# Attention queries and norm scales: which engine writes them

## The chip, the cores and the metric

The kernel runs on one core of a Trainium2 chip. A core has TensorE (PE, matrix products into PSUM), VectorE (DVE), ScalarE (ACT), GpSimd (POOL) and the queue engine SyncE (SP), each with an instruction queue of its own that it works off in order, with semaphores between them. The metric is the device time of one execution in microseconds (us). Lower is better.

## The reference

The reference is a two-layer transformer block for diffusion: 256 tokens of `x` and 256 tokens of context, model width 1024, all in float32.

- In each layer the tokens are normalized, modulated (AdaLN), and projected by one wide matrix `w_in` into four attention branches and their gates: windowed attention (8 heads of 64, 2 key heads), differential attention (4 heads of two 64-wide halves), neighbourhood attention (8 heads of 64, with a bias), and a low-rank attention (MLA, 8 heads of 64+32).
- Queries and keys of the heads are RMS-normalized per head: `y = x * rsqrt(mean(x*x) + 1e-6) * g`. The same formula normalizes the low-rank latents, the outputs of the differential branch and the tokens before each half of a layer.
- Each branch computes `softmax(q k^T * scale) v`; the four results are multiplied by `w_branch`, gated, summed and multiplied by `w_out`, and added to the tokens.
- A mixture of 16 experts follows (2 experts a token, chosen inside one of 4 groups): `(silu(x w1) * (x w3)) w2`, weighted and added.
- The last layer computes queries for the 256 tokens of `x` alone.

## The kernel before

**Numbers in two parts.** Projections keep float32 accuracy by splitting both operands into a high part (rounded to the fast float32 format, F32R) and a low part (what the rounding left), and adding three products (`mm3`, lines 284 to 288). ACT writes the high part (`whi`, line 274 or 308) and DVE, in the experts sometimes POOL, the low part by a subtraction (`wlo`, lines 275, 310, 312). There are 4 such pairs for the weights.

**Attention scores in two products.** For the windowed, differential and neighbourhood branches two heads of 64 share the 128 rows of a tile. The keys are prepared per head: 64 rows hold the high part of the head's keys and the other 64 rows hold their low part (`qk_post`, lines 761 and 762). The queries are prepared per unit (a pair of heads and 128 queries) by `heads` (lines 919 to 930). For each of the two heads, ACT writes the high part of the head's queries into the head's own 64 rows (line 927), POOL copies these 64 rows to the other 64 (line 928, through `QX` and `pmul` of line 261), and POOL writes the low part (line 929). One product of 128 rows then gives high times high plus high times low, and a second one adds low queries times high keys. The tiles rotate through 3 buffers (`qp`). There are 72 such units (16 a branch in layer 0, 8 in layer 1), hence 144 of each of the three instructions. MLA has its own form (lines 1114 and 1115), without the copy.

**One unit of attention.** PE computes the scores into two PSUM banks (line 773); DVE adds masks and finds the negated maximum (lines 778 to 785); ACT computes exp with its sum (line 787); DVE takes the reciprocal (line 792); POOL multiplies the probabilities by it (lines 810 and 856, shown as line 261 with tile `pp`); PE transposes (line 281), ACT and DVE by turns copy the result out of PSUM (lines 269 and 271), and PE multiplies by the values (lines 827 and 870).

**The norms.** `norm_heads` squares on ACT (line 711), sums on DVE (line 713), and calls `rstd_of` (lines 616 to 620): POOL computes sum times scale plus epsilon (line 618), then raises it to the power -0.5 (line 619). DVE multiplies (line 715). Where the square is summed by ACT's accumulator (lines 875, 1045, 1046, 1184, 2111), `rstd_of` stands behind ACT directly. In the output projection, `finish` does the same in two halves (lines 1381, 1382 and 1393). `rstd_of` is called 110 times, and line 1382 runs 12 times.

**Order of the work.** SP's queue, which starts the weight loads, keeps the written order. The instructions of the other engines are put in order at build time by a scheduler that goes by priority in written order and by its own estimate of each instruction's time; each engine then works off a fixed list. `run_main` (line 470) writes one branch's projection steps interleaved with the attention units of the branch before (`side`) and the norms of the heads (`posts`), so that PE has projections to do while a unit waits. Tiles of 128x512 that hold projected heads, squares and probabilities share 12 buffers (`t2`).

Of the kernel before, what the change touches and what calls it, by code (L numbers as in the profile page):

```python
# [13 lines left out]
AF = mybir.ActivationFunctionType  # L14
OP = mybir.AluOpType
# [5 lines left out]
D = 1024  # L21
# [4 lines left out]
EPS = 1e-6  # L26
# [184 lines left out]
def kernel(ctx: ExitStack, tc: tile.TileContext, a, out, dbg=None, depth=L):  # L211
# [9 lines left out]
    act = nc.scalar.activation  # L221
    V = nc.vector
    G = nc.gpsimd
# [8 lines left out]
    def psS(i):  # L232
        return psp.tile([P, 512], F32, name=f"S{i}", tag=f"S{i}", bufs=1)
# [13 lines left out]
    def t2(name="t2"):  # L247
        return gp.tile([P, 512], F32, name=name, tag="t2", bufs=BUFS["t2"])
# [4 lines left out]
    def small(n=8):  # L253
        return gp.tile([P, n], F32, name="sml", tag=f"sml{n}", bufs=16)
# [5 lines left out]
    def pmul(o, i, s, s2=1.0):  # L260
        G.tensor_scalar(o, i, s, s2, op0=OP.mult, op1=OP.mult)  # L261

    QX = lambda o, i: pmul(o, i, 1.0)
    ev = [0]

    def evac(o, i):
        ev[0] += 1
        if ev[0] % 2:
            act(o, i, AF.Copy)
        else:  # L270
            V.tensor_copy(o, i)
# [5 lines left out]
    def transposes(src, kts):  # L277

        pt = psT()
        for k, kt in enumerate(kts):  # L280
            tp(pt[:, k * P:(k + 1) * P], src[:, kt * P:(kt + 1) * P], ident)  # L281
        return pt
# [11 lines left out]
    def C(name):  # L294
        o, w = CSO[name]
        return cst[:, o:o + w]
# [318 lines left out]

    def rstd_of(ss, n, scale):
        r = small()[:, :n]
        G.tensor_scalar(r, ss, scale, EPS, op0=OP.mult, op1=OP.add)  # L618
        G.tensor_tensor(r, r, nhalf[:, :n], op=OP.pow)  # L619
        return r  # L620

# [60 lines left out]
    def attention_layer(l, T, hT):  # L682
# [24 lines left out]
        def norm_heads(x, H, hd, ct, stt, rot0):  # L707

            sq = t2("sq")
            sqv = sq[:, :H * hd].rearrange("p (h d) -> p h d", h=H)  # L710
            act(sqv, x, AF.Square)
            ss = small()
            V.tensor_reduce(ss[:, :H], sqv, axis=AX.X, op=OP.add)  # L713
            r = rstd_of(ss[:, :H], H, 1.0 / hd)
            V.tensor_tensor(x, x, r[:, :, None].to_broadcast([P, H, hd]), op=OP.mult)
            if stt is not None:
                rd = hd - rot0
                swv = sq[:, :H * rd].rearrange("p (h s d) -> p h s d", h=H, s=2)
                xr = x[:, :, rot0:].rearrange("p h (s d) -> p h s d", s=2)
                G.tensor_tensor(swv, xr[:, :, ::-1, :],  # L720
                                stt.rearrange("p (s d) -> p s d", s=2)[:, None].to_broadcast([P, H, 2, rd // 2]), op=OP.mult)
                G.tensor_tensor(x, x, ct[:, None, :].to_broadcast([P, H, hd]), op=OP.mult)
                V.tensor_tensor(x[:, :, rot0:], x[:, :, rot0:], sq[:, :H * rd].rearrange("p (h d) -> p h d", h=H), op=OP.add)
            else:
                V.tensor_tensor(x, x, ct[:, None, :].to_broadcast([P, H, hd]), op=OP.mult)
# [119 lines left out]
        def dif_slots(operands, Vt, yT):  # L845
# [20 lines left out]
            def pv(h, t):  # L866
                nb, kt0 = (4, 0) if t < 2 else (2, 2)
                po = psT()
                for b in range(nb):
                    mm(po[:, :P], PT[h, t][:, b * P:(b + 1) * P], Vt[:, kt0 + b, h * P:(h + 1) * P], start=b == 0, stop=b == nb - 1)  # L870
                o = do[:, t % 2]
                sq = t2("sq")[:, 0:P]
                ss = small()
                V.tensor_copy(o, po[:, :P])
                act(sq, o, AF.Square, accum_out=ss[:, 0:1])
                r = rstd_of(ss[:, 0:1], 1, 1.0 / P)
                V.scalar_tensor_tensor(o, o, r, S("sub"), op0=OP.mult, op1=OP.mult)
                O[h, t] = o
# [40 lines left out]
        def heads(q, k, ring):  # L919


            *qs, l0, l1 = ring[0]
            ring.append(ring.pop(0))
            ql = (l0, l1)
            for i in range(2):
                r, x = slice(i * 64, i * 64 + 64), slice(64 - i * 64, 128 - i * 64)
                act(qs[i][r], q[r], AF.Copy)
                QX(qs[i][x], qs[i][r])
                G.tensor_tensor(ql[i][r], q[r], qs[i][r], op=OP.subtract)
            return [[(i, v[i], k[i], g == 0, g == 1) for i in range(2)] for g, v in enumerate((qs, ql))]  # L930

        def stage_win():
# [31 lines left out]
            def slots():  # L964
                ring = padded()

                def ops(pi, tok, ks):
                    return heads(w["qT"].rearrange("p (b n) -> p b n", b=4)[:, pi, tok], [v[:, ks] for v in w["kT"]], ring)
                return std_slots(ops, lambda b, pi, i: w["V"][:, b, i * 64:(i + 1) * 64], y_of(0), range(4), sink=True, mask=True)
            return steps, slots  # L970

        def stage_qkv(pre, gq, gk, br):
# [20 lines left out]
            def ops(pi, tok, ks):  # L993
                return heads(w["qT"].rearrange("p (b n) -> p b n", b=4)[:, pi, tok],
                             [v.rearrange("p (b n) -> p b n", b=4)[:, pi, ks] for v in w["kT"]], w["ring"])
# [30 lines left out]
        def stage_mla():  # L1026
# [14 lines left out]
            def p1(t):  # L1041
                n = nats["ma", t]
                sq = t2("sq")
                ss = small()
                act(sq[:, :256], n[:, :256], AF.Square, accum_out=ss[:, 0:1])
                act(sq[:, 256:384], n[:, 256:384], AF.Square, accum_out=ss[:, 1:2])
                V.tensor_scalar(ss[:, 0:1], ss[:, 0:1], 0.5, None, op0=OP.mult)
                r = rstd_of(ss[:, 0:2], 2, 1.0 / P)
                V.scalar_tensor_tensor(n[:, 0:256], n[:, 0:256], r[:, 0:1], S("mqa"), op0=OP.mult, op1=OP.mult)
                V.scalar_tensor_tensor(n[:, 256:384], n[:, 256:384], r[:, 1:2], S("mkva"), op0=OP.mult, op1=OP.mult)  # L1050
                V.tensor_copy(w["kr"][:, t, :], n[:, 384:416])
# [129 lines left out]
    for t in range(4):  # L1181
        xn = t4("xn")
        ss = small()
        act(xn, xts[t], AF.Square, accum_out=ss[:, 0:1])
        r = rstd_of(ss[:, 0:1], 1, 1.0 / D)
# [56 lines left out]
    for l in range(depth):  # L1242
# [87 lines left out]
        for half in range(2):  # L1330
            for t in QT:
                pt = transposes(mt[t], range(half * 4, half * 4 + 4))
                o = [hT[i][:, half * 4:half * 4 + 4, t * P:(t + 1) * P] for i in range(2)]
# [37 lines left out]
        def finish(t, j, ps):  # L1371

            s = t // 2
            if j == 0:
                sss[t] = small()
            ss = sss[t]
            tmp, sq = t2("tmp"), t2("sq")
            cs = slice(j * 512, (j + 1) * 512)
            V.scalar_tensor_tensor(tmp, ps, 0.5, g1[s][:, cs], op0=OP.mult, op1=OP.mult)
            V.tensor_tensor(xt[t][:, cs], xt[t][:, cs], tmp, op=OP.add)  # L1380
            act(sq, xt[t][:, cs], AF.Square, accum_out=ss[:, j:j + 1])
            G.tensor_scalar(ss[:, 2 + j:3 + j], ss[:, j:j + 1], 1.0 / D, ss[:, 2:3] if j else EPS, op0=OP.mult, op1=OP.add)
            if t not in lgp:
                lgp[t] = psS(t % 2)
            pt = transposes(xt[t], range(j * 4, j * 4 + 4))
            xT = t2("xT")
            act(xT, pt, AF.Copy)
            for g in range(4):
                mm(lgp[t][32 * g:32 * g + 32, 0:P], rwA[:, j * 4 + g].rearrange("p s e -> p (s e)"), xT[:, g * P:(g + 1) * P],
                   start=j == 0, stop=j == 1, tile_position=(0, 32 * g))  # L1390
            if j == 1:
                rr[t] = ss[:, 4:5]
                G.tensor_tensor(rr[t], ss[:, 3:4], nhalf[:, 0:1], op=OP.pow)

                us, u = t2("us")[:, 0:P], lgp[t][:, P:P + NE]
                evac(us, lgp[t][:, 0:P])
                mm(u, us, C("sel")[:, s * NE:(s + 1) * NE], start=True, stop=True)
                V.scalar_tensor_tensor(lg[:, t], u, rr[t], lb[:, s], op0=OP.mult, op1=OP.add)
# [437 lines left out]
        if not last:  # L1836
# [58 lines left out]
            def one_hots(q):  # L1895
                r = []
                o = gp.tile([P, nT, P], F32R, name="OHe", tag="t2", bufs=BUFS["t2"])
                for t in range(nT):
                    V.tensor_scalar(o[:, t], C("iota2"), -BIG, rkq[:, t, q:q + 1], op0=OP.add, op1=OP.is_equal)
                    r.append(o[:, t])  # L1900
                return r
# [149 lines left out]
        for i in range(NE + 1):  # L2051
# [16 lines left out]
            if i == NE - NC and not last:  # L2068
                oht = []
                for q in range(NC):  # L2070
                    o = one_hots(q)
# [32 lines left out]
        for t in QT:  # L2104
# [5 lines left out]
            ss = small()  # L2110
            act(xn, xt[t], AF.Square, accum_out=ss[:, 0:1])
            r = rstd_of(ss[:, 0:1], 1, 1.0 / D)
            dg = t2("dg")[:, 0:P]
            V.tensor_scalar(dg, ident, r, None, op0=OP.mult)
            for half in range(2):
# [6 lines left out]
                for k in range(4):  # L2122
                    kt = half * 4 + k
                    o, i_ = hf[:, k * P:(k + 1) * P], pt[:, k * P:(k + 1) * P]
# [82 lines left out]
```

## Time and profile before

| what | value |
|---|---|
| time, median of 3 runs | 1945.32 us (1942.74 to 1946.6) |
| time of the profiled execution | 1947.77 us |
| its span, first to last instruction | 1945.7 us |
| mean granted TensorE clock | 0.961 of full speed |
| PE busy | 1782.1 us (92%), 8748 instructions |
| DVE busy | 1224.5 us (63%) |
| ACT busy | 1006.2 us (52%) |
| POOL busy | 734.3 us (38%) |

The shares are means over stages of very different kinds: attention with projections from about 50 to 600 us and from 1150 to 1600 us, the output projection and routing after that, and the experts after each. What an engine's time is worth is to be read in the stretches where PE stands idle.

### The profile page before, as it was taken

The page shows a single profiled execution, that of the slowest core. Times are in us where ns is not written, and L with a number is a line of the kernel's source. Part 1 is how long each engine was busy: PE and PEld are TensorE (multiplying, and loading weights), DVE is VectorE, ACT ScalarE, POOL GpSimd, SP SyncE. Part 2 cuts the span into 40 slices and gives each one's busy share as a digit, 9 for nine tenths or more (in the row PEclk, how much of TensorE's full clock was granted, in tenths as well). Part 3 has the DMA queues.
Part 4 walks back from the last instruction along what each step waited for, and adds up shares of the span by engine and source line. Part 5 has one row for each costly group of instructions (what it writes and reads, how often), then busy time and mean ns, then how long its engine had stood idle before and what let it go on. Part 6 is the DMA issues. An engine that isn't in the chain of part 4 may idle for free. (4 is left out here: it accounts for less than half of the span.)

```text
span 1945.7 us, 26785 instructions
## 1 busy us (share of the span) xinstructions
PE 1782.1 (92%) x8748; PEld 1249.5 (64%) x8748; DVE 1224.5 (63%) x2350; ACT 1006.2 (52%) x2201; POOL 734.3 (38%) x1066
## 2 busy tenths in 40 slices
PE   6988999999999999669998959999999998799998
PEld 5856688776667777445655447677777676456463
DVE  4657576657556646765654367866758876567563
ACT  4437566455445534446645345555645655465461
POOL 0757453536346400532322135742437630011120
PEclk9989999999999999779999979999999999899999
DMA  9341152211572347568999673446421466379995
GB/s 340 139 141 33 70 150 74 66 34 51 228 272 66 107 153 252 184 227 325 395 403 391 277 273 147 152 166 204 119 95 44 120 244 242 117 312 420 389 411 233
DMA packets 120877, 392.41 MB, mean 202 GB/s; under 512 B 12652, under 2 KB 30348, under 8 KB 93968
## 3 DMA queue, kind: packets, MB, share of 16 engines
q1 hardware_dynamic: 114832, 377.36, 53.3%
q0 software_dynamic: 3424, 8.08, 1.2%
q10 hardware_dynamic: 2464, 5.08, 0.7%
q8 instruction: 74, 1.21, 0.3%
q14 instruction: 83, 0.68, 0.1%
HBM read 379.19 MB, written 15.27 MB: 203 GB/s over the span
## 5 line engine op out<-in xcount | busy, mean ns | idle before, releaser
L287 PE MATMUL acc<-wlo,hT 128*128 128x512 f32 (+2 forms) x976 | 381.9, 391 | 2.0 <-DVE wlo L275 2.0
L288 PE MATMUL acc<-whi,hT 128*128 128x512 f32 (+2 forms) x976 | 377.4, 388 | 0.2 <-DVE hT L275 0.2
L286 PE MATMUL acc<-whi,hT 128*128 128x512 f32 (+2 forms) x976 | 361.2, 396 | 3.0 <-ACT nat L1031 1.1
L275 DVE TENSOR_TENSOR wlo<-raw,whi 128x512 fp32r<-128x512 f32 (+1 forms) x376 | 272.4, 735 | 132.5 <-ACT whi L274 128.3
L274 ACT ACTIVATE whi<-raw 128x512 fp32r<-128x512 f32 (+1 forms) x376 | 231.3, 626 | 238.8 <-PE acc L288 184.7
L312 DVE TENSOR_TENSOR wlo<-raw,whi 128x512 fp32r<-128x512 f32 x256 | 191.2, 791 | 75.1 <-ACT whi L308 74.4
L308 ACT ACTIVATE whi<-raw 128x512 fp32r<-128x512 f32 x304 | 182.8, 629 | 78.7 <-PE h L288 42.7
L286 PEld LDWEIGHTS acc<-whi,hT 128*128 128x128 f32 x976 | 182.3, 188 | 55.9 <-issue 12.0
L287 PEld LDWEIGHTS acc<-wlo,hT 128*128 128x128 f32 x976 | 183.6, 188 | 42.7 <-issue 5.2
L288 PEld LDWEIGHTS acc<-whi,hT 128*128 128x128 f32 x976 | 183.4, 188 | 36.5 <-issue 3.0
L261 POOL TENSOR_SCALAR pp<-pp,sml 128x512 f32<-128x512 f32 (+1 forms) x168 | 119.6, 722 | 133.7 <-DVE sml L792 79.6
L787 ACT ACTIVATE pp<-S,sml 128x512 f32<-128x512 f32 (+1 forms) x192 | 117.4, 613 | 93.4 <-DVE sml L782 54.4
L310 POOL TENSOR_TENSOR wlo<-raw,whi 128x512 fp32r<-128x512 f32 x48 | 63.6, 1324 | 243.5 <-ACT whi L308 187.4
L782 DVE TENSOR_REDUCE sml<-S 128x1 f32<-128x512 f32 (+1 forms) x192 | 111.6, 595 | 31.1 <-PE S L773 30.0
L619 POOL TENSOR_TENSOR sml<-sml,nhalf 128x1 f32<-128x1 f32 (+3 forms) x110 | 122.2, 1112 | 7.1
L1981 PE MATMUL hh<-raw,xh 128*64 128x512 f32 x344 | 117.0, 624 | 5.1 <-DMA raw<-in_moe_w_dram 5.1
L618 POOL TENSOR_SCALAR sml<-sml 128x1 f32<-128x1 f32 (+3 forms) x110 | 39.2, 356 | 189.4 <-DVE sml L713 109.9
L287 PE MATMUL h<-wlo,xe 128*128 128x512 f32 x256 | 106.2, 415 | 1.3 <-DVE wlo L312 0.5
L281 PE MATMUL T<-cst,pp 128*128 128x128 f32 x560 | 90.9, 285 | 13.3 <-POOL pp L261 8.2
L286 PE MATMUL h<-whi,xe 128*128 128x512 f32 x256 | 100.4, 399 | 1.7 <-ACTq L1627 1.7
L288 PE MATMUL h<-whi,xe 128*128 128x512 f32 x256 | 101.0, 395 | 0.0
L281 PEld LDWEIGHTS T<-cst,pp 128*128 128x128 f32 x560 | 68.5, 145 | 39.2 <-POOL pp L261 12.8
(441 smaller groups left out, 3417.1 us busy)
## 6 DMA issues: line engine op xcount, KB each, us to landing
raw<-in_moe_w_dram SPq DMA_DIRECT2D x133, 1024.0 KB
raw<-in_w_in_dram SPq DMA_DIRECT2D x124, 512.0 KB
raw<-in_ada_w_dram SPq DMA_DIRECT2D x48, 1024.0 KB
w<-in_moe_w_dram SPq DMA_DIRECT2D x36, 1024.0 KB
w<-in_moe_w_dram SPq DMA_DIRECT2D x60, 256.0 KB
raw<-in_w_branch_dram SPq DMA_DIRECT2D x24, 512.0 KB
raw<-in_w_out_dram SPq DMA_DIRECT2D x24, 512.0 KB
w<-in_moe_w_dram SPq DMA_DIRECT2D x16, 512.0 KB
```

Source lines behind the costliest of these rows:

```text
L261: G.tensor_scalar(o, i, s, s2, op0=OP.mult, op1=OP.mult)
L274: act(hi, src, AF.Copy)
L275: V.tensor_tensor(lo, src, hi, op=OP.subtract)
L281: tp(pt[:, k * P:(k + 1) * P], src[:, kt * P:(kt + 1) * P], ident)
L286: mm(o, s[0], whl[0], start=start, stop=False)
L287: mm(o, s[0], whl[1], start=False, stop=False)
L288: mm(o, s[1], whl[0], start=False, stop=stop)
L308: act(hi, raw, AF.Copy)
L312: V.tensor_tensor(lo, raw, hi, op=OP.subtract)
L619: G.tensor_tensor(r, r, nhalf[:, :n], op=OP.pow)
L787: act(p[:, :nk], ps[i][:, :nk], AF.Exp, bias=nm[:, i:i + 1], accum_out=nm[:, 2 + i:3 + i])
L1981: mm(hh[r:r + 64], x, wm.cols(pi, kk * 512, 512), start=k == 0, stop=k == KT - 1, tile_position=(0, r))
```

## The change

For each head, ACT writes the high part of the queries twice, to the head's own rows and to the other head's rows, both from the query tile; POOL no longer copies. POOL still writes the low part. In `rstd_of` and in `finish`, the multiplication by the scale and the addition of epsilon are issued on DVE in place of POOL; the power stays on POOL. The helper `QX` is gone.

```diff
-    QX = lambda o, i: pmul(o, i, 1.0)
...
     def rstd_of(ss, n, scale):
         r = small()[:, :n]
-        G.tensor_scalar(r, ss, scale, EPS, op0=OP.mult, op1=OP.add)
+        V.tensor_scalar(r, ss, scale, EPS, op0=OP.mult, op1=OP.add)
         G.tensor_tensor(r, r, nhalf[:, :n], op=OP.pow)
         return r
...
                 act(qs[i][r], q[r], AF.Copy)
-                QX(qs[i][x], qs[i][r])
+                act(qs[i][x], q[r], AF.Copy)
                 G.tensor_tensor(ql[i][r], q[r], qs[i][r], op=OP.subtract)
...
             act(sq, xt[t][:, cs], AF.Square, accum_out=ss[:, j:j + 1])
-            G.tensor_scalar(ss[:, 2 + j:3 + j], ss[:, j:j + 1], 1.0 / D, ss[:, 2:3] if j else EPS, op0=OP.mult, op1=OP.add)
+            V.tensor_scalar(ss[:, 2 + j:3 + j], ss[:, j:j + 1], 1.0 / D, ss[:, 2:3] if j else EPS, op0=OP.mult, op1=OP.add)
```

## Rows read from the trace of the kernel before

**Rows 1.** The page: busy time of the engines, and the granted clock by slice.
```profile
PE 1782.1 (92%) x8748; PEld 1249.5 (64%) x8748; DVE 1224.5 (63%) x2350; ACT 1006.2 (52%) x2201; POOL 734.3 (38%) x1066
...
PEclk9989999999999999779999979999999999899999
```

**Rows 2.** Windows: stretch, its length, then busy PE, PEld, DVE, ACT, POOL, clock.
```profile
119.00:147.00 28.00, 18.61 (x76) 12.54 (x74) 22.78 (x57) 13.60 (x42) 25.69 (x35) 0.70 0.11 28
147.00:164.00 17.00, 13.38 (x76) 8.63 (x75) 13.90 (x42) 15.10 (x46) 10.46 (x24) 0.90 0.05 17
...
185.00:200.00 15.00, 12.31 (x59) 8.28 (x58) 11.29 (x28) 7.69 (x24) 13.26 (x19) 0.88 0.06 22
1200.00:1222.00 22.00, 17.27 (x72) 11.39 (x72) 14.05 (x35) 15.44 (x43) 15.06 (x32) 0.84 0.01 2
...
1503.00:1517.00 14.00, 11.39 (x61) 7.38 (x62) 10.00 (x22) 9.89 (x27) 12.04 (x26) 1.00 0.04 10
```

**Rows 3.** Lines by form: shapes xcount, then busy us, mean ns, idle before.
```profile
L261 POOL TENSOR_SCALAR qp<-qp 64x128 fp32r<-64x128 f32 x144 | 55.3, 384 | 83.8 <-ACT qp L927 71.7 <-issue 2.2 <-POOL pp L261 0.7
...
L927 ACT ACTIVATE qp<-wqT 64x128 fp32r<-64x128 f32 x48 | 14.8, 308 | 15.3 <-PE S L773 9.6 <-DVE wqT L271 4.0 <-POOL sml L618 1.0
...
L785 DVE TENSOR_TENSOR sml<-sml,nsink 128x1 f32<-128x1 f32 x48 | 12.9, 277 | 0.3
...
L1047 DVE TENSOR_SCALAR sml<-sml 128x1 f32<-128x1 f32 x8 | 1.2, 150 | 1.0 <-ACT sq L1045 1.0
```

**Rows 4.** The page's costliest groups: line 618, all its shapes.
```profile
L618 POOL TENSOR_SCALAR sml<-sml 128x1 f32<-128x1 f32 (+3 forms) x110 | 39.2, 356 | 189.4 <-DVE sml L713 109.9
```

**Rows 5.** Timeline, all engines, around 131 us: start, us, instruction, idle before.
```profile
130.76 1.78 DVE L785 TENSOR_TENSOR sml<-sml,nsink 128x1 f32<-128x1 f32 x1
131.17 1.36 POOL L261 TENSOR_SCALAR pp<-pp,sml 128x512 f32<-128x512 f32 x2
131.91 1.12 PE L281 MATMUL T<-cst,pp 128*128 128x128 f32 x4 [3.89 <-POOL pp L261]
...
132.58 0.69 ACT L787 ACTIVATE pp<-S,sml 128x512 f32<-128x512 f32 x1 [4.38 <-DVE sml L785]
```

**Rows 6.** Timeline, all engines, around 1207 us.
```profile
1206.72 0.31 ACT L927 ACTIVATE qp<-wqT 64x128 fp32r<-64x128 f32 x1
...
1207.12 0.29 POOL L261 TENSOR_SCALAR qp<-qp 64x128 fp32r<-64x128 f32 x1
...
1208.86 0.45 POOL L929 TENSOR_TENSOR qp<-wqT,qp 64x128 fp32r<-64x128 f32 x1
...
1209.38 0.70 PE L773 MATMUL S<-wkv,qp 128*128 128x512 f32 x2 [2.68 <-POOL qp L929]
```

**Rows 7.** Windows of line 927 alone: busy ACT and count in the stretches.
```profile
119.00:147.00 28.00, 2.69 (x9) 0.70 0.11 28
147.00:164.00 17.00, 2.24 (x8) 0.90 0.05 17
...
185.00:200.00 15.00, 1.52 (x5) 0.88 0.06 22
1200.00:1222.00 22.00, 4.31 (x14) 0.84 0.01 2
...
1503.00:1517.00 14.00, 2.44 (x8) 1.00 0.04 10
```

**Rows 8.** Windows of line 618 alone: busy POOL and count.
```profile
119.00:147.00 28.00, 1.03 (x4) 0.70 0.11 28
...
185.00:200.00 15.00, 0.59 (x1) 0.88 0.06 22
```

**Rows 9.** Timeline, all engines, at 123 and 161 us.
```profile
123.06 0.39 PE L288 MATMUL acc<-whi,hT 128*128 128x512 f32 x1
...
161.76 2.05 ACT L908 ACTIVATE nat<-acc 128x512 f32<-128x512 f32 x4
...
164.26 0.50 PE L286 MATMUL acc<-whi,hT 128*128 128x512 f32 x1
```

## The prediction

> **What bounds the kernel now.** I read the page first. PE is busy for 92% of the span and no other engine passes 63% [rows 1], so most of what ACT, DVE and POOL do lies beside PE, and removing work from POOL (38%) is worth nothing by itself. The line of granted clocks names the first place where that is not so: of its 40 slices of 48.6 us, the third (97 to 146 us) shows 8, the only one below 9 in an attention stage; the others below 9 are routing and the change of layers [rows 1]. So I cut the attention stages, which hold the change, into windows. In most of them PE is full. In four it is not [rows 2]: 119 to 147 us (18.6 of 28 busy, granted clock 0.70 of full speed), 147 to 164 (13.4 of 17), 185 to 200 (12.3 of 15) and 1200 to 1222 (17.3 of 22). There PE has little but attention units to do. Around 123 us the last projection product ends, the evacuation of its four banks comes 38 us later on ACT, and projections go on at 164 us [rows 9]. Between them the pace is set by whichever of POOL, DVE and ACT is fullest. In the first window that is POOL (25.7 of 28, DVE 22.8, ACT 13.6); in the second ACT (15.1 of 17, POOL 10.5); in the third POOL again (13.3 of 15, DVE 11.3); in the fourth ACT and POOL are level (15.4 and 15.1 of 22).
>
> **The copies.** 144 POOL copies go, 55.3 us at a mean of 384 ns [rows 3]. 144 ACT copies come. Same shape, same kind as line 927, so 308 ns each [rows 3]: 44.4 us. The path through them becomes: ACT own rows, ACT other rows, and beside the second one POOL's subtraction, which needs only the first. By the count of line 927, each of which has one copy behind it, the four windows hold 9, 8, 5 and 14 [rows 7].
>
> **The scales.** 110 of line 618 leave POOL, 39.2 us at a mean of 356 ns [rows 4], and the 12 of line 1382, of the same kind, at that mean 4.3 us. They come to DVE as one operation on 128x1 to 128x8. The nearest row is line 1047, the same operation on 128x1: 150 ns. A small DVE operation in a crowd is line 785, mean 277 ns [rows 3]. So DVE's load grows by 18 us (122 x 0.150) to 34 us (122 x 0.277). I take 0.15 us, the same operation. Below nothing it can't be; it replaces no DVE work. Behind the 70 head norms it adds no wait, since DVE's own sum comes directly before it. Behind ACT's accumulators (lines 875, 1046, 1184, 2111, 1381: 52 of the 122) DVE now waits where POOL did, and weight splits (line 275) queue behind that wait. POOL waited there for ACT without holding anything up; DVE may hold up a split (an estimate of 0.7 us, the length that ACT's 128x512 has in rows 5). I cost it at nothing, since the order of the lists is made with that wait in view, and keep one split for each of the two output projections as the other end: 0 to +1.4 us.
>
> **The sum, window by window.** The stretch is taken to shrink with its fullest engine.
> - 119 to 147 us: POOL loses 9 x 0.384 = 3.5 us and four scales, 1.03 us [rows 8], and falls from 25.7 to 21.2. DVE, 22.8 + 4 x 0.15 = 23.4, is next. 28 x 23.4 / 25.7 = 25.5: 2.5 us saved. Bounds: nothing, if the chain from unit to unit and not POOL sets the pace; 4.5 us if what POOL loses passes on in full.
> - 147 to 164 us: ACT is the fullest, and 8 x 0.308 = 2.5 us come to its 15.1 of 17 [rows 2, 7], which makes 17.6. That is 0.6 us over; since they don't fall evenly I take 1.0 us lost. Bounds: 0 and 2.5.
> - 185 to 200 us: POOL loses 5 x 0.384 and 0.59 [rows 8], 2.5 of 13.3; DVE with 11.4 is next. By proportion 2.1 us, but PE has only 2.7 us idle there [rows 2]; I take 1.5. Bounds 0 and 2.5.
> - 1200 to 1222 us: PE waits 2.68 us for a row of eight copies and subtractions on POOL [rows 6]. ACT had written the last own rows at 1207.03. Of POOL's instructions after that (from 1207.12 to 1209.31) two are copies of 0.29 us [rows 6], and with the gaps around them POOL ends some 0.8 us earlier: 0.8 us saved. ACT there goes from 15.4 to 15.4 + 14 x 0.308 = 19.8 of 22, full but not over. Bounds: 1.5 us lost (five of the copies pushing exp back, line 787), 2 us saved.
> - Clock. In the first window PE ran at 0.70 of full speed, so a part of it at the lower level of 1.2 GHz, after the idle that starts at 123 us. 18.6 x 0.30 = 5.6 us is all that is to be had there [rows 2]. If idle goes from 9.4 to 6.9 us, about a seventh comes back: 0.8 us. Bounds 0 and 5.6.
> - Everywhere else PE has work enough [rows 1], and the copies and the scales cost nothing while it has. If that cover is gone, see the second rival.
>
> Sum: -2.5 + 1.0 - 1.5 - 0.8 - 0.8 = -4.6 us. Against the profiled execution, 1947.77 us (1945.7 of span and 2.1 around it), that makes 1943.2; that execution is 2.45 us above the median of 1945.32, so against the median it is **1940.7 us**.
>
> **A rule beside a row.** At 130.76 us DVE's smallest operation took 1.78 us in place of 0.15. It ended at 132.54, when POOL's pair of `pp` did (132.53); ACT's exp waited 4.38 us behind it and PE 3.89 us for POOL [rows 5]. The Trainium skill, "SBUF — State Buffer", section "Who interferes with whom", says that DVE and GpSimd share one pair of SBUF ports, taken as an exclusive lock for a whole instruction, by DVE operations with two SBUF inputs and also by a scalar operation in its fast mode. By that rule each copy less on POOL frees DVE as well, but the moved scale can be held up itself, for as long as a POOL operation lasts. The trace agrees for the two-input operation; for the scale it shows no such case: line 1047 stays at 150 ns, but has few POOL operations beside it [rows 3]. By the rule alone the five scales of the first and third window could cost DVE up to 1.4 us each (as long as POOL's pair of 1.36 us), and the sum would be between -4.6 and about zero: the first rival's time.
>
> **The rivals.**
> 1. *Nothing measurable.* POOL's time is freed, but the next in line, DVE, sets the pace at once: it is at 22.8 of 28 and 11.3 of 15, and takes the scales [rows 2]. If a scale there costs as much as line 785 did at 130.76 us (1.6 us over its due), 5 x 1.6 = 8 us on DVE eat what POOL gave, of which half is on the path: -4.6 + 4 = about 1944.7. For it: DVE is over 75% in both windows. Against: the copies, not the scales, are the larger part, and DVE does not take those.
> 2. *Slower: ACT becomes the bound.* Place: the attention units without projections, 147 to 164, 1200 to 1222 and 1503 to 1517 us, where ACT is at 89, 70 and 71% [rows 2]. The 30 copies there cost 30 x 0.308 = 9.2 us [rows 7]. They stand in ACT's list ahead of the next exp, and PE's next scores need the bank that this exp frees. It decides from the point where exp runs later than PE's other work lasts. With all of it exposed and the 4.0 us of the first and third window still won: 1945.3 + 9.2 - 4.0 = 1950.5. Against: ACT stays under its stretch in all but one of the three, and PE's longest idle there is POOL's [rows 6].
> 3. *Much faster through another order.* The scheduler makes all lists anew. The 38 us between the last product and the evacuation of its banks [rows 9] come from the order in which it frees `t2` tiles. If units and norms go through faster in its estimate, the evacuation comes earlier, and PE gets projections to fill the gaps: PE idle in the first three windows is 9.4 + 3.6 + 2.7 = 15.7 us [rows 2]; two thirds of it would make 1935. The same can go the other way by as much, which is in the range.
>
> **Chances and range.** 0.2% is 3.9 us, about what a measurement of this kernel can tell from no change; faster is thus below 1941.4 and slower above 1949.2. The forecast's own case, 1936 to 1943, has 0.45, of which 0.06 lies above 1941.4; rival 1 has 0.26, rival 2 0.18, rival 3 0.11. Faster: 0.39 + 0.11 = 0.50; same 0.06 + 0.26 = 0.32; slower 0.18. The range of 1930 to 1951 leaves out the far sides of rivals 2 and 3.
>
> **What would show it.** In the changed profile: no line 928 on POOL and 144 more of ACT's 64x128 casts at about 308 ns; POOL near 635 us, ACT near 1050, DVE near 1243. In 119 to 147 us POOL no longer the fullest, the wait of PE for `pp` of line 261 below 3.89 us, and the stretch up to the four evacuations of line 908 shorter by 2 to 4 us. If PE's waits for exp (line 787) grow instead, by 5 us or more over the span, rival 2 holds. If the moved scales show a mean far over 150 ns, rival 1. If the four evacuations move by 10 us or more against the projection's end, rival 3. The prediction is wrong in its mechanism if attention from 119 to 200 us is not shorter at all.

## The result, and the profile after

The changed kernel takes 1960.45 us (median of 8 runs, 1955.34 to 1964.74), the kernel before 1945.92 us (median of 8, 1942.36 to 1951.26). The ratio is 1.0076, with a 95% interval of 1.0063 to 1.0088: some 14.5 us slower by the medians, where 4.6 us faster was forecast. The profiled execution took 1964.74 us, the longest of the 8, with a span of 1962.9.

The page after, the lines that answer to [rows 1]:
```profile
PE 1794.3 (91%) x8748; PEld 1256.7 (64%) x8748; DVE 1246.7 (64%) x2472; ACT 1052.1 (54%) x2345; POOL 633.4 (32%) x800
...
PEclk8989999999999999879998979999999999799999
```
The loads came out as forecast: POOL 633 us for some 635, ACT 1052 for 1050, DVE 1247 for 1243. So the work was counted rightly, and yet the span of the profiled execution grew by 17 us. Of these, 12.2 are busy time of PE with the same 8748 matmuls, which took longer where the granted clock was lower (mean 0.954, before 0.961) or where they stood in another order; 5 are idle time.

The windows after, the three of layer 0 in [rows 2] (the two of layer 1 lie over other work by now, since that runs some 17 us later):
```profile
119.00:147.00 28.00, 17.45 (x69) 12.34 (x69) 24.37 (x58) 15.97 (x47) 19.48 (x21) 0.67 0.15 51
147.00:164.00 17.00, 11.85 (x61) 7.68 (x60) 12.92 (x40) 14.80 (x46) 7.21 (x14) 0.84 0.11 32
185.00:200.00 15.00, 14.04 (x71) 10.44 (x71) 13.00 (x30) 10.04 (x30) 9.92 (x11) 1.00 0.12 36
```
In 119 to 147 us POOL fell from 25.69 to 19.48 us and is no longer the fullest; DVE is, with 24.37, and PE did less in the same time, 17.45 us for 18.61. The stretch to the four evacuations, [rows 9] before, is now:
```profile
123.76 0.39 PE L287 MATMUL acc<-whi,hT 128*128 128x512 f32 x1
...
166.43 2.04 ACT L907 ACTIVATE nat<-acc 128x512 f32<-128x512 f32 x4
```
From the last projection product to the evacuations it is 42.7 us, before 38.7. The forecast wanted 2 to 4 us less; it is 4.0 more. This length alone doesn't tell the loss, though: in the two profiles with the scales alone on DVE (e1 below) it is 42.1 and 42.9 us, and that kernel loses nothing over the whole.

PE's waits (what was waited for, us in total, times, longest), first in a second profile of the kernel before, then after:
```profile
PE S L773 <- ACT pp L787: 8.9, 17, 1.7
PE T L281 <- POOL pp L261: 8.8, 8, 3.9
```
```profile
PE S L772 <- ACT pp L786: 20.7, 19, 6.1
...
PE T L280 <- POOL pp L261: 6.0, 7, 1.8
```
The waits for POOL's `pp`, 3.89 us at the longest [rows 5], are 1.8 us at the longest now, and the wait of 2.68 us for POOL's query tile [rows 6] is gone. In their place PE waits up to 6.09 us for an exp. The timeline after, where that wait stands (start, us, instruction, idle before), and two lines of before:
```profile
122.60 3.33 POOL L618 TENSOR_TENSOR sml<-sml,nhalf 128x8 f32<-128x8 f32 x2 [19.25 <-DVE sml L617]
...
125.91 1.25 POOL L719 TENSOR_TENSOR sq<-nat,stdkn 128x512 f32<-128x512 f32 x1
125.97 1.75 DVE L714 TENSOR_TENSOR nat<-nat,sml 128x512 f32<-128x512 f32 x1 [0.27 <-POOL sml L618]
...
127.86 1.26 POOL L719 TENSOR_TENSOR sq<-nat,stdkn 128x512 f32<-128x512 f32 x1 [0.70 <-DVE nat L714]
127.93 1.74 DVE L274 TENSOR_TENSOR wlo<-raw,whi 128x512 fp32r<-128x512 f32 x1
...
129.99 0.68 DVE L781 TENSOR_REDUCE sml<-S 128x1 f32<-128x512 f32 x1
...
130.70 0.64 DVE L784 TENSOR_TENSOR sml<-sml,nsink 128x1 f32<-128x1 f32 x1
...
131.37 0.69 ACT L786 ACTIVATE pp<-S,sml 128x512 f32<-128x512 f32 x1 [4.01 <-DVE sml L784]
...
132.21 1.22 PE L772 MATMUL S<-wkv,qp 128*128 128x512 f32 x2 [6.09 <-ACT pp L786]
```
```profile
123.20 0.69 DVE L715 TENSOR_TENSOR nat<-nat,sml 128x512 f32<-128x512 f32 x1 [0.24 <-POOL sml L619]
...
124.41 0.72 DVE L275 TENSOR_TENSOR wlo<-raw,whi 128x512 fp32r<-128x512 f32 x1
```
Read it from below: PE's scores waited for the bank that exp frees, exp for DVE's line 784, that for DVE's row maximum, and this stood behind two DVE operations of 1.75 us. Both lie beside a two-input operation of POOL that began up to 0.07 us ahead of them. Before, the same norm and the same weight split took 0.69 and 0.72 us, ahead of POOL's multiplications of the key norms (line 720 there, from 124.67 us), and the same scores waited 1.68 us, at 127.31. Now multiplications and DVE operations start together. POOL is not early here: it had waited 19.25 us for a scale that is now DVE's (line 617), and began the powers at 122.60 us, before at 119.52. So this meeting belongs to the whole change with its new lists; no copy on ACT stands in the way.

### The profile page after: what moved, and what is told of

The parts are those of the page before. It is cut to its first block, busy times and chain, and to the rows that moved or that the text cites. A ratio compares the mean times of both kernels' runs of the same rounds, so it can differ in the third digit from the quotient of the medians.

```text
span 1962.9 us, 26764 instructions
## 1 busy us (share of the span) xinstructions
PE 1794.3 (91%) x8748; PEld 1256.7 (64%) x8748; DVE 1246.7 (64%) x2472; ACT 1052.1 (54%) x2345; POOL 633.4 (32%) x800
## 5 line engine op out<-in xcount | busy, mean ns | idle before, releaser
L274 DVE TENSOR_TENSOR wlo<-raw,whi 128x512 fp32r<-128x512 f32 (+1 forms) x376 | 279.6, 752 | 141.9 <-ACT whi L273 140.2
L618 POOL TENSOR_TENSOR sml<-sml,nhalf 128x1 f32<-128x1 f32 (+3 forms) x110 | 126.9, 1159 | 219.9 <-DVE sml L617 215.7
L286 PE MATMUL acc<-wlo,yh 128*128 128x512 f32 x192 | 76.1, 397 | 0.7 <-DVE wlo L274 0.7
```

Of the source, the lines that this page charges most:

```text
L274: V.tensor_tensor(lo, src, hi, op=OP.subtract)
L286: mm(o, s[0], whl[1], start=False, stop=False)
```

## The experiments

Three theories. **A**: the copies on ACT stand between a unit's query and its exp, and PE waits for the bank (**A'**, A widened: so does load on DVE, which makes the maximum that exp waits for). **B**: the scales on DVE cost the time. **C**: any new assignment makes the scheduler write other lists, and the order alone costs it. Each run below is compared with the kernel before; us are the ratio's difference times 1946. "Attention" is the time from the first score product to the first sum of the output projection in layer 0, plus from line 1611's first addition to the last such sum in layer 1, from the first and last starts of those lines (1171.3 us before). It is read from one profile each; those of the change and of f2 are the slowest of their executions, those of e3 and f4 the fastest. "Exp" and "pp" are PE's waits as above.

| run | ratio, interval | us | attention | exp | pp |
|---|---|---|---|---|---|
| before once more (n1) | 1.0007 [0.9993, 1.0020] | +1.4 | -0.1 | 8.9 | 8.8 |
| the change | 1.0076 [1.0063, 1.0088] | +14.8 | +12.1 | 20.7 | 6.0 |
| scales only (e1) | 0.9988 [0.9976, 1.0000] | -2.3 | +1.0 | 9.6 | 5.1 |
| scales only, again | 1.0007 [0.9999, 1.0016] | +1.4 | +1.2 | 10.5 | 5.4 |
| copies only (e2) | 1.0057 [1.0042, 1.0072] | +11.1 | +9.2 | 18.4 | 7.4 |
| POOL copies from q (e3) | 1.0028 [1.0017, 1.0039] | +5.4 | -1.9 | 14.6 | 6.4 |
| copies on DVE (e4) | 1.0073 [1.0057, 1.0089] | +14.2 | +8.8 | 18.4 | 8.7 |
| *order of before:* whole change (f1) | 1.0070 [1.0055, 1.0084] | +13.6 | +8.7 | 19.8 | 4.4 |
| copies only (f3) | 1.0035 [1.0022, 1.0049] | +6.8 | +4.7 | 18.0 | 3.2 |
| scales only (f5) | 1.0033 [1.0022, 1.0044] | +6.4 | +1.9 | 11.6 | 5.9 |
| copies on DVE (f4) | 1.0082 [1.0065, 1.0099] | +16.0 | +10.1 | 18.0 | 5.3 |
| half of the copies (g5) | 1.0027 [1.0017, 1.0038] | +5.3 | +3.6 | 17.1 | 4.4 |
| copies made twice (f6) | 1.0147 [1.0133, 1.0162] | +28.6 | +23.5 | 24.8 | 5.4 |
| copies at POOL's place (g2) | 1.0028 [1.0012, 1.0044] | +5.4 | +2.6 | 16.9 | 5.1 |
| copies behind exps (g3) | 1.0057 [1.0041, 1.0072] | +11.1 | +9.6 | 16.8 | 6.3 |
| the same, later (g4) | 1.0078 [1.0064, 1.0092] | +15.2 | +12.9 | 15.4 | 5.7 |
| *work of before* in the order of e2 (f2) | 1.0039 [1.0024, 1.0053] | +7.6 | +4.8 | 13.2 | 10.8 |

**What a difference of nothing looks like** (n1): the kernel before, no edit.

> The kernel before once more, against itself: what a difference of nothing looks like. Ratio 1.000 within 0.0015 either way. Its profile shows which differences between profiles are chance: by theory C and A alike the first 96 us (no copy and no attention yet) differ by chance, up to the 3 us that the profiles so far show there; the stage from the first scores of the last attention of layer 0 to its output projection should be 187.6 us again within 0.5.

The ratio holds 1, and attention is 1171.2 us against 1171.3. The two profiles of e1, one kernel too, agree within 0.2 us in the sum, but their layer 0 differs by 2.9 us one way and layer 1 by 2.7 the other. So the attention column tells some 1 us apart as a sum, and not by layer. The start of the program differed by 0.8 us between n1 and the kernel before, the experts of layer 0 by 2.7 and those of layer 1 by 6.3.

**Parts alone, order free** (e1, its repetition, e2):
```
-        G.tensor_scalar(r, ss, scale, EPS, op0=OP.mult, op1=OP.add)
+        V.tensor_scalar(r, ss, scale, EPS, op0=OP.mult, op1=OP.add)
...
-            G.tensor_scalar(ss[:, 2 + j:3 + j], ss[:, j:j + 1], ...
+            V.tensor_scalar(ss[:, 2 + j:3 + j], ss[:, j:j + 1], ...
```


> Only the scales move to DVE; the 144 copies stay on POOL. Theory A (ACT's added copies delay exp and PE's scores wait for its bank): within 4 us of the kernel before, and PE's wait for exp (line 787) near the 9.0 us of before. Theory B (the scales on DVE cost the time, by making DVE wait for ACT's accumulators): 8 to 15 us slower, exp waits near 9 us all the same. Theory C (any new assignment makes a new order of all lists, and the order alone costs some us): anything within 10 us, and this run and the one with only the copies do not add up to the +14.6 us of the whole change.

> The scales alone on DVE in the free order once more, the only version so far below the kernel before: 2 us faster than before if the first run (0.9988) was no chance, equal to it within 2 us if it was.


```
-                QX(qs[i][x], qs[i][r])
+                act(qs[i][x], q[r], AF.Copy)
```


> Only the copies move to ACT; the scales stay on POOL. Theory A: 8 to 18 us slower than before, PE's waits for exp 15 us or more in all (9.0 before, 20.7 after), and attention of layer 0 (scores of the first unit to the output projection's first product) 4 us or more longer. Theory B: within 4 us of before. Theory C: anything within 10 us, without adding up with the scales-only run.

The scales alone change nothing that can be measured (0.9988, then 1.0007): theory B falls for the free order. The copies alone bring 11.1 of the 14.8 us and nearly the same waits for exp (18.4 and 20.7). That is what A wanted, but C could do it too.

**Copies without a load on ACT, order free** (e3, e4):
```
-                QX(qs[i][x], qs[i][r])
+                QX(qs[i][x], q[r])
```


> The copy stays on POOL but reads the query instead of ACT's result, so that it waits for nothing of ACT; no engine's load changes. Theory A: 0 to 4 us faster, since a unit's two copies on POOL can start some 0.35 us earlier and nothing is added to ACT. Theory B: the same. Theory C: it differs from before by more than 4 us in either direction, although no engine got any work more.


```
-                QX(qs[i][x], qs[i][r])
+                V.tensor_copy(qs[i][x], q[r])
```


> The copies go to DVE (144, an estimate of 0.15 to 0.28 us each, 22 to 40 us of load), scales stay on POOL. Theory A (it is ACT's list ahead of exp that costs): not slower than before by more than 4 us, since ACT gets nothing, PE's waits for exp within 4 us of the 9.0 us of before. Theory A' (any engine that is loaded between a unit's query and its exp costs: DVE makes the row maximum that exp waits for): 5 to 15 us slower. Theory C: anything within 10 us.

Both miss what A expected. In e3 no engine has other work than before, and it is 5.4 us slower: that points to the order (its profiled run was the fastest of its 12, so its attention column says little). In e4 ACT has nothing added, and the loss is as great as with ACT (a copy on DVE took 283, 334 and 441 ns on average in the three branches, up to well over the estimated 0.28 us).

**The order held.** From here on a kernel is traced twice. The lists of the first trace give each instruction a rank; in the second, with other work, each engine's instructions (SP's apart) are chained by rank with dependencies that carry no semaphore, each added copy right behind its cast:
```
+                    at = rank[i.name]
+                    if i.engine != was[i.name]:
+                        if "act" in work and i.engine == _mybir.EngineType.Activation or "dve" in work:
+                            at = rank[traced[k - 1].name] + 0.5
...
+                    row.sort(key=lambda i: pos[i.name])
+                    for p, q in zip(row, row[1:]):
+                        tc.add_manual_dep(q, p.name, nosync, reason="order")
...
+    order = build(ORDER_OF)[2]
+    nc, arrays, _ = build(WORK_OF, order)
```
With ORDER_OF the kernel before, WORK_OF was both parts (f1), the copies (f3), the copies on DVE (f4), the scales (f5); with ORDER_OF the copies-only kernel, WORK_OF was the kernel before (f2).

> The whole change, but every engine keeps the order of before: PE, and all work that isn't moved, stand in the lists as they did; each added copy on ACT stands right behind its cast, each scale on DVE where the list of before had reached it. Theory A (load: 144 copies on ACT stand ahead of exps): slower than before by 8 to 18 us, exp waits of PE 15 us or more. Theory C (the new order of the lists, not the load): within 4 us of before or faster, down to the 4.6 us of gain that the prediction had summed up, exp waits near 9 us.

> Only the copies move to ACT, in the order of before: PE's and DVE's lists are the same as before, instruction for instruction. With a free order this cost 11 us. Theory A: the 11 us stay (8 to 14 slower). Theory C: they go (within 4 us of before, or faster by up to 5).

> The work of before (copies and scales on POOL) in the order that the lists took when the copies went to ACT: ACT has none of the copies, POOL's stand ahead of their subtractions. Theory A: near the kernel before (within 4 us), since ACT's load is that of before. Theory C: slower than before by 8 to 16 us, as with the copies moved, though no engine's load has changed; more if POOL, with its copies back, is late in that order.

> The copies on DVE instead of ACT, in the order of before: PE's and ACT's lists are the same as before. With a free order this cost 13 us. Theory A' (load on any engine between query and exp): the 8 to 16 us stay. Theory C: within 4 us of before or faster.

> Only the scales on DVE, in the order of before: PE's and ACT's lists are those of before, instruction for instruction. With a free order this was 2.3 us faster. If load on DVE between scores and exp costs as load on ACT does (theory A widened), 2 to 8 us slower; the difference of the two earlier runs in the old order, with and without the scales, was 6.3. If the scales cost nothing by themselves, within 3 us of before.

Neither theory is right alone. With the order of before the copies still cost 6.8 us (A alone wanted 8 to 14, C alone under 4); with the work of before the new order costs 7.6. Both intervals lie above zero. Together they cost 11.1; whether that is less than the sum, 14.4, the intervals don't tell. In the order of before the scales cost 6.4 us, and the two parts add up (6.8 + 6.4 = 13.2, measured 13.6); in a free order the scales cost nothing in sum, whether because they find a free place or because the new lists win elsewhere what they cost. Copies on DVE cost more than on ACT, 16.0 us. So it is not ACT in particular: DVE makes the maximum that exp waits for, ACT the exp, and POOL was the one engine that is not on the way from scores to exp.

Where the order costs can be read in the last attention of layer 0, where the granted clock is 1.00 throughout. (Its units run from 574 to 670 us, past the 600 us given above for layer 0.) In the traces 4.9 other matmuls stand on average between the first and the last score product of one of its 16 units before, 14.6 in the copies-only kernel and in the change. The windows of that stretch, from its first score product to the output projection's first sum, in n1, f3, f2 and e2 (stretch, length, PE, PEld, DVE, ACT, POOL, clock):
```profile
573.00:761.00 188.00, 185.87 (x911) 144.11 (x904) 108.91 (x196) 87.47 (x201) 64.84 (x96) 1.00 0.39 129
```
```profile
579.00:767.00 188.00, 185.59 (x909) 143.73 (x909) 109.24 (x196) 95.19 (x228) 55.96 (x70) 1.00 0.38 128
```
```profile
575.00:766.00 191.00, 187.90 (x916) 144.90 (x915) 113.58 (x197) 88.34 (x202) 62.80 (x96) 1.00 0.39 128
```
```profile
577.00:769.00 192.00, 188.09 (x918) 145.10 (x916) 111.88 (x197) 96.79 (x228) 55.50 (x70) 1.00 0.38 126
```
With the order of before it takes 188 us, with the copies on ACT (f3, ACT 95.19) as without (n1, ACT 87.47). With the new order it takes 191 to 192 (190.7 and 191.3 between the two starts), with the copies (e2) as without (f2). Here the load costs nothing and the order 3 to 4 us, of which two thirds are busy time of PE (188 for 186).

Where the load costs is read in f3, whose PE list is that of before instruction for instruction, so that each wait can be laid beside its own. At 294 us in n1, and the same instructions in f3:
```profile
294.02 0.63 ACT L927 ACTIVATE qp<-dqT 64x128 fp32r<-64x128 f32 x2
...
294.68 0.47 ACT L787 ACTIVATE pp<-S,sml 128x256 f32<-128x256 f32 x1
...
295.38 0.70 PE L773 MATMUL S<-dkT,qp 128*128 128x512 f32 x2
```
```profile
299.54 0.29 ACT L927 ACTIVATE qp<-dqT 64x128 fp32r<-64x128 f32 x1
...
299.86 0.31 ACT L929 ACTIVATE qp<-dqT 64x128 fp32r<-64x128 f32 x1
...
300.19 0.31 ACT L927 ACTIVATE qp<-dqT 64x128 fp32r<-64x128 f32 x1
...
300.52 0.31 ACT L929 ACTIVATE qp<-dqT 64x128 fp32r<-64x128 f32 x1
...
300.86 0.47 ACT L787 ACTIVATE pp<-S,sml 128x256 f32<-128x256 f32 x1
...
301.47 0.72 PE L773 MATMUL S<-dkT,qp 128*128 128x512 f32 x2 [0.62 <-ACT pp L787]
```
Two casts stood ahead of this exp; now two casts and two copies (line 929 there) do. The exp starts 1.32 us after the first cast instead of 0.66, and PE, which had no wait to show there, waits 0.62 us.

And where POOL was the bound, a gain came and was given back. The place of [rows 5] in n1, then the same instructions in f3:
```profile
125.21 0.72 DVE L275 TENSOR_TENSOR wlo<-raw,whi 128x512 fp32r<-128x512 f32 x1
...
125.72 0.71 PE L773 MATMUL S<-wkv,qp 128*128 128x512 f32 x2 [1.48 <-ACT pp L787]
...
128.10 0.70 PE L773 MATMUL S<-wkv,qp 128*128 128x512 f32 x2 [1.68 <-ACT pp L787]
...
132.70 1.12 PE L281 MATMUL T<-cst,pp 128*128 128x128 f32 x4 [3.89 <-POOL pp L261]
...
134.20 0.80 PE L773 MATMUL S<-wkv,qp 128*128 128x256 f32 x2 [0.38 <-ACT pp L787]
```
```profile
127.53 2.95 POOL L720 TENSOR_TENSOR sq<-nat,stdkn 128x512 f32<-128x512 f32 x2
127.66 1.70 DVE L275 TENSOR_TENSOR wlo<-raw,whi 128x512 fp32r<-128x512 f32 x1
...
128.09 0.72 PE L773 MATMUL S<-wkv,qp 128*128 128x512 f32 x2 [1.39 <-ACT pp L787]
...
131.43 1.22 PE L773 MATMUL S<-wkv,qp 128*128 128x512 f32 x2 [2.62 <-ACT pp L787]
...
134.08 1.11 PE L281 MATMUL T<-cst,pp 128*128 128x128 f32 x4 [1.43 <-POOL pp L261]
...
136.54 0.69 ACT L787 ACTIVATE pp<-S,sml 128x512 f32<-128x512 f32 x1 [3.58 <-DVE sml L785]
...
137.37 0.79 PE L773 MATMUL S<-wkv,qp 128*128 128x256 f32 x2 [2.18 <-ACT pp L787]
```
The wait for POOL falls from 3.89 to 1.43 us, but 2.5 us are not saved by that, since the scores before it already wait 2.62 us for exp, in n1 1.68. Counted from the first scores shown, the product comes after 5.99 us in place of 6.98: 1.0 us won. The last scores shown then wait 2.18 us for exp, in n1 0.38, and come after 9.28 us in place of 8.48: 0.8 us lost in the end. Neither loss is at a copy; exp waited for DVE. POOL, with no copy to do, begins its multiplication (line 720) 0.13 us ahead of DVE's weight split, which then takes 1.70 us; in n1 it began 0.25 us behind it, and the split took 0.72. Such meetings add little over the whole: with the same list of work DVE is busy for 779.2 us of attention in f3 and 777.6 in n1.

**More and fewer copies** (f6: each copy on ACT made twice; g5: those of the second head only, the others stay on POOL; both in the order of before):
```
+                    act(qs[i][x], q[r], AF.Copy)
```


> The copies on ACT in the order of before, each made twice (288 copies of 0.31 us instead of 144; the second one repeats the first). Theory A (load on ACT): the loss against before doubles, from about 7 to 12 to 18 us, and PE's waits for exp go from 18 to over 25 us. If a copy on ACT costs nothing in itself and only its place or the freed POOL matters: 5 to 9 us, as with one copy.


```
-                if "act" in WORK:
+                if "act" in WORK and i:
```


> The copies of one head of each pair on ACT (72), those of the other stay on POOL, in the order of before. With 0, 144 and 288 copies on ACT in this order the loss was 0, 6.8 and 28.4 us. If each copy costs the same: 3.4 us. If copies cost only where ACT's slack ahead of an exp is used up (theory A): under 2.5 us, or even a gain up to 2 us, since POOL's row of two copies and two subtractions is halved.

With 0, 72, 144 and 288 copies on ACT the loss is 0, 5.3, 6.8 and 28.6 us: neither in proportion nor free at first. Theory A missed g5, the equal price of 3.4 us lies at the edge of its interval (3.3 to 7.4 us), and f6 is far over what either allowed. The two waits fit a reading, which no run isolated. Half of the copies already trades one wait for the other (pp 8.8 to 4.4, exp 8.9 to 17.1 us): POOL is relieved, and the way over DVE and ACT is at once the bound. The second 144 copies of f6 relieve nothing more (pp 5.4, f3 3.2), and half of their 144 x 0.308 = 44 us is lost: 28.6 - 6.8 = 21.8 us.

**The copies set back** (g2: where the lists stood when POOL issued the copy; g3 and g4: behind the last exp that stands 20 or 8 places ahead of the product that needs it; the edit of g2, then that of g3 and g4, with LEAD 20 and 8):
```
-                            at = rank[traced[k - 1].name] + 0.5
+                            at = rank[i.name]
```
```
-                            at = rank[traced[k - 1].name] + 0.5
...
+                            due = min(rank[j.name] for j in mms[:2]) - LEAD
+                            at = rank[traced[k - 1].name]
+                            at = max([at] + [rank[e] + 1 for e in EXPS if at < rank[e] + 1 < due]) + 0.5
```


> Only the copies on ACT, in the order of before, but each copy stands where the lists had come to when POOL issued it, not right behind its cast (some 28 copies move). Theory A (place ahead of exp): about the 6.8 us of loss of the copies behind their casts, or some 2 us less; if the load alone counts, 5 to 9 us.

> Only the copies on ACT, in the order of before, each copy set back behind the last exp that stands at least 20 places (of all engines' lists together) before the first score product that needs it; some 126 of 144 move. Theory A (a copy costs because it stands ahead of an exp): the loss falls from 6.8 us to 0 to 4 us, PE's waits for exp from 18 towards 9 us. If ACT's load alone counts: 5 to 9 us of loss as before.

> The same with 8 places in place of 20, so that copies stand behind more exps but nearer to the score product that needs them. Theory A: as with 20 places, 0 to 4 us of loss, unless PE then waits for the copies themselves (its waits for the query tile grow), which would bring it to 4 to 10 us.

This part of theory A fell. Behind the exps the copies cost more, 11.1 and 15.2 us, and the waits for exp hardly went down (16.8, 15.4). In g4 PE also waits for the copies themselves, 2.9 us. So its place right ahead of an exp is not what a copy costs by; that it then delays ACT's other work (ACT is busy for 14.80 of 17 us in 147 to 164 after) is the reading left, but no run isolated it. g2 (5.4) can't be told from f3 (6.8).

**What stays open.** f5's 6.4 us: its attention is only 1.9 us longer; its first scores come 2.3 us later than n1's, which may be chance (see the end), and the rest was not located. No run kept POOL as busy as before while the copies ran on ACT, so what a POOL that comes sooner costs is not told apart from what the copies cost. And the timed loss of most versions is 1 to 7 us over the loss in attention; one profile each doesn't say whether that lies at the start and in the experts. No version was clearly faster than the kernel before.

## Why the prediction was wrong

**Right**: the counts and loads (above); 308 ns for a copy on ACT (measured 308 to 309); that POOL's 3.89 us wait would shrink; that POOL would no longer be the fullest. The moved scales cost less than could have been, by form after:
```profile
L617 DVE TENSOR_SCALAR sml<-sml 128x8 f32<-128x8 f32 x34 | 8.5, 250 | 0.5
L617 DVE TENSOR_SCALAR sml<-sml 128x4 f32<-128x4 f32 x28 | 5.2, 185 | 0.3
L617 DVE TENSOR_SCALAR sml<-sml 128x1 f32<-128x1 f32 x32 | 4.8, 150 | 6.7 <-ACT sq L874 4.2 <-ACT xn L1183 2.3
L617 DVE TENSOR_SCALAR sml<-sml 128x2 f32<-128x2 f32 x16 | 2.9, 181 | 0.6
```
The 128x1 form is 150 ns, the value taken. All 110 together are 21.4 us, with the 12 of line 1381 23.6, inside the 18 to 34 for 122, so rival 1's mark, a mean far over 150 ns, was not met (193). For the rule weighed in the prediction the trace now has cases: of these 110, 60 had no POOL work beside them and took 173 ns at most; of the 50 beside POOL, 9 took over 400 ns, up to 1136, one of them here:
```profile
140.28 1.35 POOL L261 TENSOR_SCALAR pp<-pp,sml 128x512 f32<-128x512 f32 x2
...
140.53 1.14 DVE L617 TENSOR_SCALAR sml<-sml 128x8 f32<-128x8 f32 x1
```
It ended at 141.67, POOL's pair at 141.63. The Trainium skill, "SBUF — State Buffer", section "Who interferes with whom", says that a scalar operation of DVE, too, can take the port pair that DVE shares with GpSimd, in its two-port mode, and that whoever comes second is blocked for the whole instruction. The trace agrees, though for 9 of 50. None of the 9 has one column: in the five profiles with the scales on DVE 40 operations of 128x1 ran beside POOL, and the longest took 156 ns. Line 1047, from which the price was taken, has that one shape, and so could not show the case.

**Wrong, the step that failed first**: "Everywhere else PE has work enough [rows 1], and the copies and the scales cost nothing while it has." PE's share of 92% [rows 1] was read as cover. But in attention PE's next scores need a bank that only exp frees, and PE's list is fixed: other work that would be ready stands behind. Attention grew by 12.1 us. Of these 3.0 lie between the first scores and line 1129 (96 to 246 us before), which holds the windows of [rows 2] in layer 0; 4.7 lie in the rest of layer 0's attention, which the sum had at nothing, and 4.4 in layer 1 (one profile each, whose layers can differ by 2.9 us).

With the order held the place of the loss can be read directly. f1, the whole change, has PE's list of before, so each matmul can be laid beside its own; before, then f1:
```profile
204.70 0.40 PE L286 MATMUL acc<-whi,hT 128*128 128x512 f32 x1
...
300.14 0.39 PE L287 MATMUL acc<-wlo,yh 128*128 128x512 f32 x1
```
```profile
204.38 0.39 PE L286 MATMUL acc<-whi,hT 128*128 128x512 f32 x1
...
305.93 0.39 PE L287 MATMUL acc<-wlo,yh 128*128 128x512 f32 x1
```
How much later the same matmul starts than before (us):

| matmul, start before | 119.19 | 164.26 | 204.70 | 300.14 | 573.32 | 1200.02 | 1222.83 | 1560.01 |
|---|---|---|---|---|---|---|---|---|
| f1 | 2.04 | 3.64 | -0.32 | 5.79 | 7.05 | 9.23 | 7.62 | 11.95 |
| n1 | 0.80 | 0.77 | -0.40 | -0.34 | 0.63 | 3.73 | 2.67 | 3.39 |

Over the stretches that hold the windows of the sum f1 gains: 2.4 us from 119 to 205, 1.6 from 1200 to 1223 (n1, by chance, 1.2 and 1.1). It loses 6.1 us from 205 to 300 and 4.3 from 1223 to 1560 (n1 nothing and 0.7), where the sum had put nothing. From 205 to 300 PE had been busy for 91.84 of 95.44 us and had waited for no exp. With the copies alone moved (f3) the same matmuls take 99.2 us, 0.5 of the added 3.7 busy time of PE: PE now waits there 1.3 us for exp, and 3.4 in place of 2.5 for ACT's copies out of PSUM. In f1 3.1 of the added 6.1 are busy time of PE, at a granted clock of 0.97, before 1.00. So work enough for PE was no cover, because its list stops at the first product whose release is late.

**Wrong, the terms for 119 to 200 us** (-2.5, +1.0, -1.5; and -0.8 for the clock). In the order of before the copies made the stretch up to the evacuations 0.6 us longer (39.3 for 38.7), the scales 0.9 shorter (37.8), both 1.0 longer (39.7). From the next projection product (164.26) up to 205 f1 wins 4.0 us; 3.0 of them are busy time of PE (34.65 us for 37.67), at a granted clock of 1.00 there, before 0.92 (n1 wins 1.2 us, at 0.96). In the first window, where the sum put its gain, the clock gave nothing: 0.67 in the change, before 0.70. What POOL gave up to the evacuations was passed to DVE and ACT at once. That was the lower bound, "nothing, if the chain from unit to unit and not POOL sets the pace": [rows 5] had shown exp waiting 4.38 us at the very place, for DVE, beside PE's 3.89 for POOL. Two waits of nearly the same length side by side: taking one away leaves the other.

**Rival 2's sign came true, its place and price did not, its cause in part.** Its mark was 5 us more of waits for exp; it is 11.8 more. But the mark doesn't point to ACT alone: with the copies on DVE it is 9.1 more (f4), and some of it replaces waits for POOL (pp and query tile together 11.5 us in n1, 6.0 after). It had 30 copies in three windows for 9.2 us and 1950.5. Copies outside those windows cost too, as the one at 299 us in f3, and so did the new order, which it left out.

**Rival 3 was given the wrong sign.** The order did move, and that of the copies-only kernel costs 7.6 us by itself (f2; that of the whole change was not run alone). "The same can go the other way by as much, which is in the range" stood there, but as much is 10 us, and the range ended at 1951, 6 us up; with rival 2 beside it that was too little. Its mark, evacuations that move by 10 us, didn't show: they moved by 4.0, and the order cost in the last attention instead.

## What to carry to other kernels

Ask of each engine whether it lies on the way from one unit's start to the release that the next unit needs. Here that way is scores on PE, maximum on DVE, exp on ACT; a POOL copy that looks slow (384 ns for 308) lies beside it, and moved to either of the others it costs time though they are busy half to two thirds of the span. Where two engines are waited for side by side, relief of one is worth at most the time by which its wait outlasts the other's. And where a scheduler writes the lists, test a move twice, with its own new order and with the old one held: here, for the copies, load alone lost 6.8 us, order alone 7.6, and both together 11.1.

## What the runs showed beyond that

- A two-input DVE operation on 128x512 took 0.69 to 0.72 us by itself (123.20, 124.41 before) and 1.70 to 1.75 where POOL's 128x512 had begun up to 0.13 us ahead of it (125.97, 127.93 after; 127.66 in f3). Relieving POOL can slow DVE, since POOL's next work moves beside other work of DVE, as in f3.
- The granted clock differs where the work does not. In f5 and n1, whose PE lists are the same, the stretch from 25 to 31 us of the program's start, ahead of all attention:
```profile
25.00:31.00 6.00, 5.19 (x43) 2.49 (x40) 2.23 (x8) 2.13 (x4) 0.00 (x0) 0.53 1.09 352
```
```profile
25.00:31.00 6.00, 5.48 (x55) 4.07 (x55) 3.60 (x13) 2.13 (x4) 0.00 (x0) 1.00 1.08 352
```
  At nearly the lower level of 1.2 GHz (0.53) PE shows 43 matmuls in these 6 us, at 2.4 GHz (1.00) 55, and f5 reaches its first scores at 99.2 us, n1 at 96.9. All five profiles with the scales on DVE reach them at 98.1 us or later; the other thirteen between 96.1 and 99.3. Whether the scales cause it was not tested.
